# Keys, queries and the pooling's inputs made with x stationary and turned by DMA, the pooling's product and the gate weights in wider matmuls, and the last mixing slab later

## The chip, the core and the metric

One core of a Trainium2 chip runs the kernel. The metric is the device time of one execution in microseconds (us), median of three runs: 1546.35 us before (1546.16 to 1546.65). Some 0.2% of that, 3.1 us, is about what a measurement can tell from no change.

## What is computed

One layer on x of 256 tokens by 2048 channels, in float32. One input projection feeds three branches and their gates; each branch is projected, gated, summed, projected again, and normalised with x:

```python
proj = x @ w_in                        # 2048 -> pu, pz, sx, sz, sB, sC, sdt, mq, mk, mv, mo, mz, mi, mf, gates
y_pool  = pool_mixer(pu, w_pool, pool_scale) * silu(pz)
y_ssm   = mamba2_branch(sx, sz, sB, sC, sdt, ...)
y_mlstm = mlstm_branch(mq, mk, mv, mo, mi, mf, mz, ...)
g = sigmoid(gates + b_gate)            # 3 x 2048 per token
merged = sum(g[b] * (y[b] @ w_branch[b]) for b in range(3))
out = layer_norm(ALPHA * x + merged @ w_out)
```

The pooling has four groups of 512 channels. Group g takes the causal mean over w = 2, 4, 8 or 16 tokens less the token itself, and multiplies it with a 512 x 512 matrix of its own (w_pool). The mLSTM has eight heads of 256 channels, done here in four pairs, and needs keys and queries with channels on the partitions.

## The kernel before

All weights stream from HBM once, in an order written out by `stream()`; nearly all of the work is the product of x (256 tokens) or of a branch's output with slabs of 512 weight columns by 2048 rows (16 steps k of 128 rows). Each float32 operand is split into a high and a low float32r part: ScalarE (ACT) casts the high part (`split`, L190), VectorE (DVE) subtracts for the low part (L191), and TensorE (PE) sums high x high, high x low and low x high. The weights are split in parts of 1024 elements per partition, two steps k of a 512-column slab or four of a 256-column half. Four such parts fit (`hpool`, 4 buffers), so ACT and DVE may run up to four parts ahead of PE, and no further. Each engine works its own queue strictly in order.

There are two ways to make a slab. `slab_tok` (L262 to L264) keeps 128 tokens of x stationary and streams 512 weight columns: per k and token tile three matmuls of 512 columns, 96 in a slab; tokens come out on the partitions. `slab_chan` (L280 to L299) keeps 128 weight columns stationary: per k and block a matmul of 256 columns (low weights, L286) and one of 512 (high weights, high and low x side by side, L291), 128 in a slab; channels come out on the partitions, and ACT and DVE add the two halves (L298, L299). Before, keys and queries (`mlstm`) and the pooling's pu and pz (`pool`) are made by `slab_chan`, 16 slabs, and so are six slabs of the SSM branch. `slab_pool` (L301) mixes a pooling group in 48 matmuls of 256 columns and two PSUM tiles. `prep` makes the 48 small gate columns in 48 matmuls of 256 columns (L379 to L381).

Work beside the slabs is written as generators in the queue `pending`. `pump()` advances the oldest generator by one step; a slab calls it after every part, and whatever the step issues goes into the engines' queues there. `turned_parts` is such a generator: ACT copies a [256 x 512] float32 tile into its two 16-bit planes (L334, two copies), ACT issues two DMA transposes (L337), DVE puts the planes together again (L345, four copies), and the result is split. It runs seven times before (four mLSTM outputs, three merged tiles).

The PSUM pool `acc` has four tiles of one bank. A slab takes two of them, and gets a tile only when its last reader is done. The SBUF pool `big` has 11 tiles (names `t`).

In `pool`, group g makes pu (`slab_chan`), pools it on DVE (L698 adds, doubling the window each time, so 1, 2, 3 and 4 adds for the four groups; then L704 to L707), makes pz (`slab_chan`, then Silu), splits the pooled tile, and then mixes the group before it (`mix`, `slab_pool`, L684 on DVE). The last group is mixed at the end of `pool`, ahead of the merge's first gate slab.

Of the kernel before, what the change touches and what calls it, by code (L numbers as in the profile page):

```python
# [9 lines left out]
F32 = mybir.dt.float32  # L10
# [5 lines left out]
P = 128  # L16
# [22 lines left out]
def stream():  # L39


    def tok(c0, j):
        return [("w_in", 0, c0 + j * CB, CB, KT)]

    def chan(c0, j):
        return [("w_in", 0, c0 + j * CB + c, HB, KT) for c in (0, HB)]

    def merge(b):
        order = tok(GATES + b * D, 0)
        for j in range(NB):  # L50
            if j + 1 < NB:
                order += tok(GATES + b * D, j + 1)
            order.append(("w_branch", b, j * CB, CB, KT))
        return order

    order = tok(SZ, 0) + chan(SB_, 0) + chan(SC_, 0) + chan(SX, 0)
    for g in range(1, 4):
        order += tok(SZ, g) + chan(SX, g)
    order += merge(1)
    for g in range(4):  # L60
        order += chan(MK, g) + chan(MQ, g) + tok(MV, g) + tok(MO, g) + tok(MZ, g)
    order += merge(2)
    for g in range(4):
        order += chan(PU, g) + chan(PZ, g)
        if g:
            order.append(("w_pool", g - 1, 0, CB, CB // P))
    order.append(("w_pool", 3, 0, CB, CB // P))
    order += merge(0)
    order += [("w_out", 0, j * CB, CB, KT) for j in range(NB)]
    return order  # L70

# [6 lines left out]
def trunk(  # L78
# [31 lines left out]
    def nm(s):  # L110
        uid[0] += 1
        return f"{s}_{uid[0]}"
# [28 lines left out]
    def bank():  # L141
        return mx.tile([P, 512], F32, tag="mx", name=nm("mx"))
# [46 lines left out]
    def split(h, l, src):  # L189
        A.copy(h, src)  # L190
        V.tensor_sub(l, src, h)  # L191
# [64 lines left out]
    def yparts(ys):  # L256
        return lambda k: (ys[k // 4][0][:, k % 4, :], ys[k // 4][1][:, k % 4, :])
# [8 lines left out]
    def slab_tok(parts=xparts, first=False):  # L266
# [34 lines left out]
    def slab_pool(ph, pl):  # L301

        nk = CB // P
        ps = [acc.tile([P, 2, S], F32, tag="acc", name=nm("acc")) for _ in range(2)]
        for k, wh, wl in w_parts(nk):
            h, l = ph[:, k, :], pl[:, k, :]
            for c in range(4):
                o = ps[c // 2][:, c % 2, :]
                m = slice(c * P, (c + 1) * P)
                nc.tensor.matmul(o, lhsT=wh[:, m], rhs=h, start=k == 0 and c % 2 == 0, stop=False, skip_group_check=True)  # L310
                nc.tensor.matmul(o, lhsT=wh[:, m], rhs=l, start=False, stop=False, skip_group_check=True)  # L311
                nc.tensor.matmul(o, lhsT=wl[:, m], rhs=h, start=False, stop=k == nk - 1, skip_group_check=True)  # L312
            if k % 2 == 1:
                pump()
        return ps

    def transposed_parts(src_of, yh, yl):

# [5 lines left out]
            A.copy(yh[:, :, c], pt)  # L324
            V.tensor_sub(yl[:, :, c], pt, yh[:, :, c])

    def turned_parts(src, planes, yh, yl):
# [12 lines left out]
        yield  # L340
        f = planes.rearrange("p t c -> p (t c)").rearrange("p (a s) -> p a s", a=4)
        fv = f.bitcast(U16).rearrange("p a (t c h) -> p h t a c", t=NT, h=2)
        for i in range(2):
            for t in range(NT):
                V.tensor_copy(fv[:, i, t], dv[:, i, t])  # L345
            yield
        A.copy(yh, f)
        V.tensor_sub(yl, f, yh)

    def y_tiles():  # L350
        return (ypool.tile([P, 4, S], F32R, tag="yh", name=nm("yh")),
# [17 lines left out]
        return tiny.tile([P, NT, 40], F32, tag="s80", name=nm("s80"))  # L369

    def prep():
        wsh, wsl = t4([KT, 48], F32R), t4([KT, 48], F32R)
        split(wsh, wsl, wsm)
        yield
        yield
        yield
        pz = bank()[0:48, 0:S]
        for k in range(KT):
            nc.tensor.matmul(pz, lhsT=wsh[:, k, :], rhs=xh[:, k, :], start=k == 0, stop=False)  # L379
            nc.tensor.matmul(pz, lhsT=wsh[:, k, :], rhs=xl[:, k, :], start=False, stop=False)  # L380
            nc.tensor.matmul(pz, lhsT=wsl[:, k, :], rhs=xh[:, k, :], start=False, stop=k == KT - 1)  # L381
        zr = t2([S])
        A.copy(zr[0:48, :], pz)
        yield
        yield
        pzt = bank()[:, 0:96].rearrange("p (t c) -> p t c", t=NT)
        for t in range(NT):
            nc.tensor.transpose(pzt[:, t, :], zr[0:48, t * P:(t + 1) * P], ident[0:48, 0:48])
        V.tensor_tensor(out=zz, in0=pzt, in1=rowb[:, 0:48].unsqueeze(1).broadcast_to([P, NT, 48]), op=ALU.add)
# [257 lines left out]
    def mlstm():  # L647
        ys = []
        dw, dw1 = [t4([4, S]), t4([4, S])], t4([NM, P])
        pending.append(ml_weights(dw, dw1))  # L650
        for hp in range(4):
            kt, qt = t4([4, S]), t4([4, S])
            slab_chan(kt, MD ** -0.5)
            slab_chan(qt)
            ps = slab_tok()
            vh, vl = t4([NT, 2, MD + 2], F32R), t4([NT, 2, MD + 2], F32R)
            one = ones[:, 0:NT * 2 * 2].rearrange("p (t h d) -> p t h d", t=NT, h=2)
            V.tensor_copy(vh[:, :, :, MD:MD + 2], one)
# [12 lines left out]
            V.tensor_tensor(out=sz, in0=sz, in1=nw.unsqueeze(1).broadcast_to([P, NT, CB]), op=ALU.mult)  # L671
            pending.append(ml_pair(hp, kt, qt, vh, vl, so, sz, dw, dw1, ys))
        return ys


    def pool():
        ys = []
        pend = []

        def mix(g, ph, pl, sp):  # L680
            ps = slab_pool(ph, pl)
            yf = t4([4, S])
            for c in range(4):
                V.scalar_tensor_tensor(out=yf[:, c, :], in0=ps[c // 2][:, c % 2, :], scalar=pscale[:, 4 * g + c:4 * g + c + 1],  # L684
                                       in1=sp[:, c, :], op0=ALU.mult, op1=ALU.mult)
            yh, yl = y_tiles()
            split(yh, yl, yf)
            ys.append((yh, yl))

        for g, w in enumerate(WINDOWS):  # L690
            u = t4([4, 272])
            V.memset(u[:, :, 0:16], 0.0)
            slab_chan(u[:, :, 16:272])
# [6 lines left out]
            sp = t4([4, S])  # L700
            slab_chan(sp)
            A.activation(sp, sp, AF.Silu)
# [5 lines left out]
            ph, pl = t4([4, S], F32R), t4([4, S], F32R)  # L708
            split(ph, pl, p)
            if pend:  # L710
                mix(*pend.pop())
            pend.append((g, ph, pl, sp))
        mix(*pend.pop())
        return ys


    merged = []
# [7 lines left out]
        A.activation(sg, sg, AF.Sigmoid)  # L725
        return sg

    def merge(b, ys, done=None):
        sg = gate(b, 0)
        for j in range(NB):  # L730
            nxt = gate(b, j + 1) if j + 1 < NB else None
            ps = slab_tok(yparts(ys))
            if len(merged) <= j:
                m = ypool.tile([P, NT, CB], F32, tag="m", name=nm("m"))
# [23 lines left out]
            transposed_parts(lambda t, i: m[:, t, i * P:(i + 1) * P], mh, ml)  # L758
        yield

    merge(0, pool(), finish)


    st = const.tile([P, NT, 2 * NB, 6], F32, name="st")
# [146 lines left out]
```

## Time and profile before

| | before |
|---|---|
| median of 3 runs | 1546.35 us (1546.16 to 1546.65) |
| the profiled execution | 1545.71 us, of which the span from first to last instruction is 1543.8 us |
| PE busy | 1535.6 us, 99% of the span, 7727 matmuls |
| DVE busy | 964.8 us, 62% |
| ACT busy | 725.8 us, 47% |
| granted TensorE clock | 0.999 of 2.4 GHz |
| DMA | 305.35 MB, mean 198 GB/s |

Busy time of PE overlaps its neighbours in the records, since one matmul begins before the record of the last ends; the distance from one matmul's start to the next is what it costs. Waits of an engine are idle time before an instruction, put down to what came last.

### The profile page before, as it was taken

The page shows a single profiled execution, that of the slowest core. Times are in us where ns is not written, and L with a number is a line of the kernel's source. Part 1 is how long each engine was busy: PE and PEld are TensorE (multiplying, and loading weights), DVE is VectorE, ACT ScalarE, POOL GpSimd, SP SyncE. Part 2 cuts the span into 40 slices and gives each one's busy share as a digit, 9 for nine tenths or more (in the row PEclk, how much of TensorE's full clock was granted, in tenths as well). Part 3 has the DMA queues.
Part 4 walks back from the last instruction along what each step waited for, and adds up shares of the span by engine and source line. Part 5 has one row for each costly group of instructions (what it writes and reads, how often), then busy time and mean ns, then how long its engine had stood idle before and what let it go on. Part 6 is the DMA issues. An engine that isn't in the chain of part 4 may idle for free.

```text
span 1543.8 us, 19035 instructions
## 1 busy us (share of the span) xinstructions
PE 1535.6 (99%) x7727; PEld 1302.3 (84%) x7727; DVE 964.8 (62%) x1230; ACT 725.8 (47%) x818; POOL 13.6 (1%) x38
## 2 busy tenths in 40 slices
PE   9999999999999999999999999999999999999998
PEld 7888888888888888888888888888888898888886
DVE  5858888755754465465475466455666685556666
ACT  6545545544544444444444454443544454444441
POOL 0000000000000000000000000000000000000001
PEclk9999999999999999999999999999999999999999
DMA  8545555645655545546556556555555555566752
GB/s 316 192 168 187 208 189 187 229 173 191 218 191 192 191 172 205 195 173 210 196 182 208 191 204 212 199 197 196 188 191 189 191 191 191 193 224 213 273 198 99
DMA packets 70711, 305.35 MB, mean 198 GB/s; under 512 B 20280, under 2 KB 29152, under 8 KB 36832
## 3 DMA queue, kind: packets, MB, share of 16 engines
q1 hardware_dynamic: 55264, 299.69, 54.3%
q10 hardware_dynamic: 15360, 4.46, 1.6%
q8 instruction: 60, 0.98, 0.2%
q14 instruction: 27, 0.22, 0.0%
HBM read 298.32 MB, written 2.14 MB: 195 GB/s over the span
## 4 chain that ended last, share of the span: by engine, by line
PE 99%; DMA 1%; DVE 0%; issue 0%; DVEq 0%; SPq 0%
PE acc L291 21%; PE acc L262 21%; PE acc L264 21%; PE acc L263 21%; PE acc L286 11%; PE mx L527 1%; PE acc L312 0%; PE acc L311 0%; PE acc L310 0%; PE mx L597 0%; DMA w<-in_wt_dram 0%; PE mx L322 0%; DMA xf<-in_xT_dram 0%; PE mx L599 0%; PE mx L503 0%; PE mx L520 0%
## 5 line engine op out<-in xcount | busy, mean ns | idle before, releaser
L191 DVE TENSOR_TENSOR wl<-w,wh 128x1024 fp32r<-128x1024 f32 (+1 forms) x538 | 654.5, 1220 | 500.1 <-ACT wh L190 498.3
L190 ACT CAST wh<-w 128x1024 fp32r<-128x1024 f32 (+1 forms) x538 | 562.2, 1047 | 682.0 <-PE acc L264 449.6
L291 PE MATMUL acc<-xhl,wh 128*128 128x512 f32 x1408 | 488.2, 392 | 0.0
L286 PE MATMUL acc<-xhl,wl 128*128 128x256 f32 x1408 | 387.9, 281 | 0.0
L262 PE MATMUL acc<-wh,xhl 128*128 128x512 f32 x896 | 350.5, 391 | 0.3 <-ACT wh L190 0.3
L263 PE MATMUL acc<-wl,xhl 128*128 128x512 f32 x896 | 349.1, 390 | 0.2 <-DVE wl L191 0.2
L264 PE MATMUL acc<-wh,xhl 128*128 128x512 f32 x896 | 349.1, 390 | 0.1
L291 PEld LDWEIGHTS acc<-xhl,wh 128*128 128x128 f32 x1408 | 262.1, 188 | 54.3
L286 PEld LDWEIGHTS acc<-xhl,wl 128*128 128x128 f32 x1408 | 264.6, 188 | 3.5
L262 PEld LDWEIGHTS acc<-wh,xhl 128*128 128x128 f32 x896 | 168.2, 188 | 35.6 <-ACT wh L190 1.2
L264 PEld LDWEIGHTS acc<-wh,xhl 128*128 128x128 f32 x896 | 168.2, 188 | 35.5 <-DVE xhl L191 0.4
L263 PEld LDWEIGHTS acc<-wl,xhl 128*128 128x128 f32 x896 | 168.3, 188 | 35.3 <-DVE wl L191 1.0
L262 PE MATMUL acc<-wh,yh 128*128 128x512 f32 x384 | 149.7, 390 | 0.0
L264 PE MATMUL acc<-wh,yl 128*128 128x512 f32 x384 | 149.5, 389 | 0.0
L263 PE MATMUL acc<-wl,yh 128*128 128x512 f32 x384 | 149.5, 389 | 0.0
L264 PEld LDWEIGHTS acc<-wh,yl 128*128 128x128 f32 x384 | 72.1, 188 | 15.0
L262 PEld LDWEIGHTS acc<-wh,yh 128*128 128x128 f32 x384 | 72.1, 188 | 14.9
L263 PEld LDWEIGHTS acc<-wl,yh 128*128 128x128 f32 x384 | 72.1, 188 | 14.9
L298 ACT ACTIVATE t<-acc 128x256 f32<-128x256 f32 x88 | 31.8, 383 | 51.9 <-PE acc L291 51.9
L262 PE MATMUL acc<-wh,t 128*128 128x512 f32 (+1 forms) x144 | 52.7, 366 | 0.0
L264 PE MATMUL acc<-wh,t 128*128 128x512 f32 (+1 forms) x144 | 52.7, 366 | 0.0
L263 PE MATMUL acc<-wl,t 128*128 128x512 f32 (+1 forms) x144 | 52.6, 366 | 0.0
(202 smaller groups left out, 835.0 us busy)
## 6 DMA issues: line engine op xcount, KB each, us to landing
w<-in_wt_dram SPq DMA_DIRECT2D x264, 1024.0 KB, 4.8
t<-sc_a SPq DMA_DIRECT2D x8, 512.0 KB, 7.7
w<-in_wt_dram SPq DMA_DIRECT2D x6, 512.0 KB, 7.7
t<-in_b_gate_dram SPq DMA_DIRECT2D x12, 256.0 KB, 4.7
h<-in_x_dram SPq DMA_DIRECT2D x4, 512.0 KB, 4.8
xf<-in_xT_dram SPq DMA_DIRECT2D x7, 256.0 KB, 7.5
out_dram<-h SPq DMA_DIRECT2D x5, 256.0 KB, 2.5
w<-in_wt_dram SPq DMA_DIRECT2D x4, 256.0 KB, 4.8
```

The source lines that it names most:

```text
L190: A.copy(h, src)
L191: V.tensor_sub(l, src, h)
L262: nc.tensor.matmul(o, lhsT=h[:, c], rhs=wh, start=first, stop=False)
L263: nc.tensor.matmul(o, lhsT=h[:, c], rhs=wl, start=False, stop=False)
L264: nc.tensor.matmul(o, lhsT=l[:, c], rhs=wh, start=False, stop=last)
L286: nc.tensor.matmul(ps[c][:, 0, :], lhsT=wl[:, m], rhs=xh[:, k, :], start=False, stop=False, skip_group_check=True)
L291: nc.tensor.matmul(ps[c], lhsT=wh[:, m], rhs=xhl[:, k], start=first, stop=last, skip_group_check=True)
L298: A.mul(o, ps[c][:, 1, :], scale)
L527: nc.tensor.matmul(py[:, h * HP:(h + 1) * HP], lhsT=lt[c][:, h, :], rhs=xd[:, c, h, :], start=True, stop=True)
```

## The change

Keys and queries of each pair of heads, and pu and pz of each pooling group, are made by `slab_tok`; ACT copies PSUM to SBUF (`slab_turned`; pz goes through Silu there), and the generator `turned` turns the tile to channels on the partitions by way of two DMA transposes. The pz slab pumps after every k (`dense`), twice as often as before. The pooling of a group becomes a generator, `windows`, which runs during the pz slab. `slab_pool` takes high and low of the pooled tile side by side, as `slab_chan` does with x: 32 matmuls in place of 48, all four k for one block of 128 columns and then the next, in four PSUM tiles in place of two. `prep` keeps the high and low gate weights side by side as 96 stationary columns: 32 matmuls in place of 48, and one more add. The mixing of the last group moves from the end of `pool` to behind the merge's second gate slab, and its weights move in the stream with it.

```diff
     for g in range(4):
-        order += chan(MK, g) + chan(MQ, g) + tok(MV, g) + tok(MO, g) + tok(MZ, g)
+        order += tok(MK, g) + tok(MQ, g) + tok(MV, g) + tok(MO, g) + tok(MZ, g)
...
-            if k % 2 == 1:
+            if k % 2 == 1 or dense:
                 pump()
...
+    def slab_pool(phl, use):
         nk = CB // P
+        ws = list(w_parts(nk))
+        for c in range(4):
+            ps = acc.tile([P, 2, S], F32, tag="acc", name=nm("acc"))
+            m = slice(c * P, (c + 1) * P)
+            for k, wh, wl in ws:
+                hl = phl[k // 2][:, k % 2]
...
+                nc.tensor.matmul(ps, lhsT=wh[:, m], rhs=hl, start=k == 0, stop=k == nk - 1, skip_group_check=True)
...
+            use(c, ps)
...
+    def slab_turned(scale=1.0, func=AF.Copy, dense=False):
+        ps = slab_tok(dense=dense)
+        src, planes = t4([NT, CB]), t4([NT, CB])
+        for t in range(NT):
+            A.activation(src[:, t, :], ps[t], func, scale=scale)
+        return src, planes
...
         for hp in range(4):
-            kt, qt = t4([4, S]), t4([4, S])
-            slab_chan(kt, MD ** -0.5)
-            slab_chan(qt)
+            kq = []
+            for scale in (MD ** -0.5, 1.0):
+                src, planes = slab_turned(scale)
+                kq.append(by_channel(planes))
+                pending.append(turned(src, planes, kq[-1]))
...
+            def use(c, ps):
+                o, w = yf[:, c, :], pscale[:, 4 * g + c:4 * g + c + 1]
+                A.copy(o, ps[:, 1, :])
+                V.tensor_add(o, ps[:, 0, :], o)
+                V.scalar_tensor_tensor(out=o, in0=o, scalar=w, in1=sp[:, c, :], op0=ALU.mult, op1=ALU.mult)
...
+        for g, w in enumerate(WINDOWS):
+            phl, ready = [], []
+            pending.append(windows(w, slab_turned(), phl))
+            zs = slab_turned(func=AF.Silu, dense=True)
+            pending.append(gates(*zs, ready))
             if pend:
                 mix(*pend.pop())
```

Three places show what moves. The first is ACT's queue at the end of the last pz slab, where the third group is mixed (names `t` are SBUF tiles, `acc` PSUM tiles, `wh` weight parts). Before:

```order
L298 ACTIVATE t_1530_9766<-acc_9857 128x256
L298 ACTIVATE t_1530_9766<-acc_9858 128x256
L190 CAST wh_10057<-w_10027 128x1024
L702 ACTIVATE t_1530_9766<-t_1530_9766 128x1024
L190 CAST wh_10100<-w_10098 128x1024
L190 CAST wh_10116<-w_10098 128x1024
```

and now:

```order
L191 CAST wh_9506<-w_9504 128x1024
L191 CAST t_1544_9403<-t_1540_9387 128x2x256
L191 CAST t_1545_9412<-t_1540_9387 128x2x256
L369 ACTIVATE t_1548_9431<-acc_9265 128x512
L369 ACTIVATE t_1548_9431<-acc_9266 128x512
L191 CAST wh_9523<-w_9504 128x1024
L715 COPY t_1550_9435<-acc_9446 128x256
L342 COPY t_1549_9432<-t_1548_9431 128x1024 x2
L715 COPY t_1550_9435<-acc_9458 128x256
L345 DMA_TRANSPOSE t_1548_9431<-t_1549_9432 128x8x128
L715 COPY t_1550_9435<-acc_9471 128x256
L345 DMA_TRANSPOSE t_1548_9431<-t_1549_9432 128x8x128
```

The readers of the slab's PSUM tiles (L369) now stand behind the split of the pooled tile, and the readers of the mixing's PSUM tiles (L715) between copies and transposes; one more L715 and the cast of the next part follow.

The second is DVE's queue in the last pz slab (window 16). Before, each add stood between two weight parts:

```order
L698 TENSOR_TENSOR t_1526_9758<-t_1501_9576 128x4x271
L191 TENSOR_TENSOR wl_9834<-w_9811,wh_9833 128x1024
L698 TENSOR_TENSOR t_1527_9760<-t_1526_9758 128x4x269
L191 TENSOR_TENSOR wl_9862<-w_9859,wh_9861 128x1024
L698 TENSOR_TENSOR t_1528_9762<-t_1527_9760 128x4x265
```

and now they come after the copies that wait for the transposes:

```order
L352 COPY t_1523_9279<-t_1516_9261 128x4x128 x2
L192 TENSOR_TENSOR wl_9370<-w_9347,wh_9369 128x1024
L352 COPY t_1523_9279<-t_1516_9261 128x4x128 x2
L192 TENSOR_TENSOR wl_9394<-w_9391,wh_9393 128x1024
L732 TENSOR_TENSOR t_1531_9345<-t_1523_9279 128x4x271
L732 TENSOR_TENSOR t_1535_9359<-t_1531_9345 128x4x269
L192 TENSOR_TENSOR wl_9416<-w_9391,wh_9415 128x1024
L732 TENSOR_TENSOR t_1536_9367<-t_1535_9359 128x4x265
L192 TENSOR_TENSOR wl_9439<-w_9436,wh_9438 128x1024
L732 TENSOR_TENSOR t_1539_9379<-t_1536_9367 128x4x257
L192 TENSOR_TENSOR wl_9443<-w_9436,wh_9442 128x1024
```

The copies stand one part behind their transposes here, and two adds share one part.

The third is PE's queue in a mixing slab, one block of 128 columns. Before:

```order
L310 MATMUL acc_9956<-t_1489_9503,wh_9960 128x256
L311 MATMUL acc_9956<-t_1490_9504,wh_9960 128x256
L312 MATMUL acc_9956<-t_1489_9503,wl_9961 128x256
```

for each k and block; now the whole of a block is

```order
L318 MATMUL acc_9446<-t_1473_9008,wh_9438 128x512
L313 MATMUL acc_9446<-t_1473_9008,wl_9439 128x256 x2
L318 MATMUL acc_9446<-t_1473_9008,wh_9438 128x512
L313 MATMUL acc_9446<-t_1477_9023,wl_9443 128x256
L318 MATMUL acc_9446<-t_1477_9023,wh_9442 128x512
L313 MATMUL acc_9446<-t_1477_9023,wl_9443 128x256
L318 MATMUL acc_9446<-t_1477_9023,wh_9442 128x512
L318 MATMUL acc_9458<-t_1473_9008,wh_9438 128x512
```

and the next block takes the next PSUM tile.

## Rows read from the trace of the kernel before

**Rows 1.** The page: busy time of each engine, and the chain that ended last.

```profile
PE 1535.6 (99%) x7727; PEld 1302.3 (84%) x7727; DVE 964.8 (62%) x1230; ACT 725.8 (47%) x818; POOL 13.6 (1%) x38
...
PE 99%; DMA 1%; DVE 0%; issue 0%; DVEq 0%; SPq 0%
```

**Rows 2.** Waits: engine, tile and line, what it waited for, total us, times, longest.

```profile
ACT wh L190 <- PE acc L264: 449.6, 273, 3.8
...
ACT wh L190 <- PE acc L291: 158.1, 100, 2.8
...
PE mx L154 <- DVE warm L151: 1.3, 1, 1.3
...
PE mx L812 <- ACT t L810: 0.9, 1, 0.9
```

**Rows 3.** Windows of a chan slab, a tok slab, and half a chan slab with a mixing.

```profile
core 0: us, PE busy (x) PEld busy (x) DVE busy (x) ACT busy (x) POOL busy (x), PEclk, DMA share, GB/s
1187.02:1209.21 22.19, 22.19 (x130) 19.54 (x129) 17.16 (x19) 10.59 (x13) 0.00 (x0) 1.00 0.53 186
1314.28:1336.04 21.76, 21.76 (x97) 18.02 (x97) 11.00 (x12) 9.39 (x9) 0.00 (x0) 1.00 0.54 193
1209.21:1226.06 16.85, 16.85 (x114) 15.52 (x113) 10.92 (x14) 8.90 (x10) 0.00 (x0) 1.00 0.51 189
```

**Rows 4.** One line of `prep`: duration in ns, first and last start in us.

```profile
L380 PE MATMUL mx<-xhl,t x16: 276/276/279, 76.1 to 81.2; 128*48 128x256 f32 x16
```

**Rows 5.** ACT in order of time around three pairs of DMA transposes (start, us).

```profile
582.18 1.05 ACT L190 CAST wh<-w 128x1024 fp32r<-128x1024 f32 x1
582.31 2.73 ACTq L337 DMA_TRANSPOSE t<-t  x2
585.13 1.05 ACT L190 CAST wh<-w 128x1024 fp32r<-128x1024 f32 x1 [1.90 <-issue]
...
926.97 3.33 ACTq L337 DMA_TRANSPOSE t<-t  x2
...
1340.51 1.05 ACT L190 CAST wh<-w 128x1024 fp32r<-128x1024 f32 x1
1340.63 4.73 ACTq L337 DMA_TRANSPOSE m<-t  x2
1345.40 3.06 ACT L190 CAST wh<-w 128x1024 fp32r<-128x1024 f32 x3 [3.85 <-PE acc L264]
```

**Rows 6.** DVE in order of time: the copies behind these transposes.

```profile
589.86 1.47 DVE L345 COPY t<-t 128x512 uint16<-128x512 uint16 x4 [0.62 <-DMA t<-t]
...
936.71 1.47 DVE L345 COPY t<-t 128x512 uint16<-128x512 uint16 x4 [4.05 <-DMA t<-t]
...
1347.63 0.47 DVE L345 COPY t<-m 128x512 uint16<-128x512 uint16 x1
```

**Rows 7.** DMA issues by line: KB or kind, median us to landing.

```profile
t<-t ACTq DMA_TRANSPOSE x8, 5.9
...
m<-t ACTq DMA_TRANSPOSE x6, 5.6
```

**Rows 8.** DVE in order of time in the third pu and pz slabs.

```profile
1188.24 1.29 DVE L698 TENSOR_TENSOR t<-t 128x1084 f32<-128x1084 f32 x1
1189.44 1.22 DVE L191 TENSOR_TENSOR wl<-w,wh 128x1024 fp32r<-128x1024 f32 x1
1190.58 1.27 DVE L698 TENSOR_TENSOR t<-t 128x1076 f32<-128x1076 f32 x1
...
1197.91 1.18 DVE L704 SCALAR_TENSOR_TENSOR t<-t,t 128x992 f32<-128x992 f32 x1
```

**Rows 9.** Groups of instructions: count, busy us, mean ns, idle before.

```profile
L298 ACT ACTIVATE t<-acc 128x256 f32<-128x256 f32 x88 | 31.8, 383 | 51.9 <-PE acc L291 51.9
...
L334 ACT COPY t<-t 128x1024 uint16<-128x1024 uint16 x8 | 8.0, 1044 | 4.2 <-DVE t L640 4.1
...
L190 ACT CAST xhl<-xf 128x512 fp32r<-128x512 f32 (+1 forms) x10 | 5.2, 530 | 2.1 <-DMA xf<-in_xT_dram 2.0
...
L552 ACT ACTIVATE t<-acc 128x512 f32<-128x512 f32 x8 | 4.7, 597 | 4.1 <-PE acc L264 3.9
```

More of the change, by code (lines that the diff above doesn't have):

```diff
@@ L46, in chan, with merge @@
         return [("w_in", 0, c0 + j * CB + c, HB, KT) for c in (0, HB)]
-    def merge(b):
+    def merge(b, between=()):
         order = tok(GATES + b * D, 0)
@@ L52, in merge @@
                 order += tok(GATES + b * D, j + 1)
+            if j == 0:
+                order += between
             order.append(("w_branch", b, j * CB, CB, KT))
@@ L264, in mm_tok, with slab_tok @@
         nc.tensor.matmul(o, lhsT=l[:, c], rhs=wh, start=False, stop=last)
-    def slab_tok(parts=xparts, first=False):
+    def slab_tok(parts=xparts, first=False, dense=False):
         ps = [acc.tile([P, CB], F32, tag="acc", name=nm("acc")) for _ in range(NT)]
@@ L299, in slab_chan, with low @@
                 V.scalar_tensor_tensor(out=o, in0=ps[c][:, 0, :], scalar=scale, in1=o, op0=ALU.mult, op1=ALU.add)
-    def slab_pool(ph, pl):
+    def slab_pool(phl, use):
         nk = CB // P
[L304 to L313, printed above, removed]
+        ws = list(w_parts(nk))
[4 more added lines that the diff above has]
+                hl = phl[k // 2][:, k % 2]
+                def low():
+                    nc.tensor.matmul(ps[:, 0, :], lhsT=wl[:, m], rhs=hl[:, 0, :], start=False, stop=False,
+                                     skip_group_check=True)
+                if k:
+                    low()
+                nc.tensor.matmul(ps, lhsT=wh[:, m], rhs=hl, start=k == 0, stop=k == nk - 1, skip_group_check=True)
+                if not k:
+                    low()
+            use(c, ps)
+            if c % 2 == 1:
                 pump()
-        return ps
     def transposed_parts(src_of, yh, yl):
@@ L346, in turned_parts, with by_channel @@
             yield
+    def by_channel(t):
+        return t.rearrange("p t c -> p (t c)").rearrange("p (a s) -> p a s", a=4)
+    def turned_parts(src, planes, yh, yl):
+        f = by_channel(planes)
+        yield from turned(src, planes, f)
         A.copy(yh, f)
         V.tensor_sub(yl, f, yh)
+    def slab_turned(scale=1.0, func=AF.Copy, dense=False):
[4 more added lines that the diff above has]
+        return src, planes
     def y_tiles():
@@ L371, in prep @@
     def prep():
-        wsh, wsl = t4([KT, 48], F32R), t4([KT, 48], F32R)
-        split(wsh, wsl, wsm)
+        ws = [t4([KT // 2, 2, 48], F32R) for _ in range(2)]
+        for i, w in enumerate(ws):
+            split(w[:, :, 0, :], w[:, :, 1, :], wsm[:, i * KT // 2:(i + 1) * KT // 2, :])
         yield
@@ L678, in pool, with mix @@
         pend = []
-        def mix(g, ph, pl, sp):
-            ps = slab_pool(ph, pl)
+        def mix(g, phl, sp, ready):
+            assert ready
             yf = t4([4, S])
-            for c in range(4):
-                V.scalar_tensor_tensor(out=yf[:, c, :], in0=ps[c // 2][:, c % 2, :], scalar=pscale[:, 4 * g + c:4 * g + c + 1],
-                                       in1=sp[:, c, :], op0=ALU.mult, op1=ALU.mult)
+            def use(c, ps):
[3 more added lines that the diff above has]
+                V.scalar_tensor_tensor(out=o, in0=o, scalar=w, in1=sp[:, c, :], op0=ALU.mult, op1=ALU.mult)
+            slab_pool(phl, use)
             yh, yl = y_tiles()
@@ L688, in mix, with windows @@
             ys.append((yh, yl))
-        for g, w in enumerate(WINDOWS):
+        def windows(w, us, phl):
             u = t4([4, 272])
             V.memset(u[:, :, 0:16], 0.0)
-            slab_chan(u[:, :, 16:272])
+            yield from turned(*us, u[:, :, 16:272])
             s, n = u, 1
@@ L707, in pool, with gates @@
             V.tensor_sub(p[:, :, 0:w], p[:, :, 0:w], u[:, :, 16:16 + w])
-            ph, pl = t4([4, S], F32R), t4([4, S], F32R)
-            split(ph, pl, p)
+            yield
+            for i in range(2):
+                t = t4([2, 2, S], F32R)
+                phl.append(t)
+                split(t[:, :, 0, :], t[:, :, 1, :], p[:, 2 * i:2 * i + 2, :])
+                yield
+        def gates(src, planes, ready):
+            yield from turned(src, planes, by_channel(planes))
+            ready.append(True)
+        for g, w in enumerate(WINDOWS):
[3 more added lines that the diff above has]
+            pending.append(gates(*zs, ready))
             if pend:
                 mix(*pend.pop())
-            pend.append((g, ph, pl, sp))
-        mix(*pend.pop())
-        return ys
+            pend.append((g, phl, by_channel(zs[1]), ready))
+        return ys, lambda: mix(*pend.pop())
     merged = []
@@ L726, in gate, with merge @@
         return sg
-    def merge(b, ys, done=None):
+    def merge(b, ys, done=None, between=None):
         sg = gate(b, 0)
@@ L731, in merge @@
             nxt = gate(b, j + 1) if j + 1 < NB else None
+            if j == 0 and between is not None:
+                between()
             ps = slab_tok(yparts(ys))
@@ L759, in finish @@
         yield
-    merge(0, pool(), finish)
+    ys, last = pool()
+    merge(0, ys, finish, last)
     st = const.tile([P, NT, 2 * NB, 6], F32, name="st")
```

34 lines of the change are left out of this document (17 added, 17 removed).

## The prediction

> **What bounds the kernel now.** I read the page's first part and its chain first: PE is busy 99% of the span and holds 99% of the chain that ended last [rows 1]. Then the waits: PE waits a few microseconds in all, the longest of them at the start (1.3 us) and in the last normalisation (0.9 us), while ACT waits 449.6 + 158.1 us for PE to give a buffer of split weights back [rows 2]. So the weights are ready early, and the time is the sum of the distances between matmuls. Whatever takes matmul time out is gained in full, as long as PE still never waits. How long PE can be left alone follows from the four split buffers: a buffer comes back three parts before its next use, a part of a 512-column slab lasts 21.76 / 8 = 2.72 us [rows 3], and the cast and the subtraction take 1.05 and 1.22 us [rows 5, 8]; so a part lies ready about 3 x 2.72 - 1.05 - 1.22 = 5.9 us before PE needs it (an estimate from those rows). A delay on ACT or DVE below that costs nothing; a PSUM tile that is read late costs at once.
>
> **What PE saves.** The profiled execution took 1545.71 us, 0.64 us under the median of 1546.35; the sum is made in it and laid on the median.
>
> A slab with weight columns stationary takes 22.19 us, one with x stationary 21.76 us, both windows holding nothing else on PE [rows 3]. Both stream the same columns, and the first has 128 matmuls against 96, so each matmul has a fixed part. Sixteen slabs change: 16 x 0.43 = 6.9 us. The same code makes 28 such slabs already, so I see no reason for another price; 6.5 to 7.2 us.
>
> A mixing takes 16.85 - 22.19 / 2 = 5.76 us [rows 3]. Its new step, a matmul of 512 and one of 256 columns with a new stationary operand each, is what the 22.19 us slab consists of 64 times: 0.347 us. Sixteen steps are 5.55 us; four mixings save 0.8 us.
>
> `prep`: the second of its three matmuls starts from 76.1 to 81.2 us, sixteen times, so three take 5.1 / 15 = 0.34 us and one 0.113 us [rows 4]. Sixteen go: 1.8 us. The 96-column ones may cost up to the 0.12 us of a mixing's matmul (5.76 / 48), which takes 0.1 us back.
>
> Together 9.5 us, with ends 8.8 and 9.9. Without any new wait the median is 1536.9 us.
>
> The Trainium skill speaks against this first term: "TensorE: Matmul & The Clock Gate", section Back-to-back issue gap, gives N / 2.4 + 2.5 ns for the distance of matmuls at full clock. By that a 512-column matmul takes 215.8 ns and a slab 20.7 us in either form, and the sixteen slabs would save 1.3 us in all. The trace disagrees: 21.76 / 96 is 227 ns.
>
> **What is added, and what covers it.** 16 slabs get a turn each: on ACT two copies of 1.04 us [rows 9] and two issues of a DMA transpose, on DVE four copies of 1.47 us together [rows 6], against the four PSUM reads on either engine that go. Averaged over 21.76 us both engines have room: in the window of the tok slab DVE is busy 11.00 and ACT 9.39 us [rows 3]. What counts is how long a turn holds a queue. ACT's next cast came 2.8, 3.4 and 4.8 us after the first of two transposes (the third: 1345.40 - 1340.63) [rows 5], and DVE's copies began 7.5, 9.7 and 7.0 us after it [rows 5, 6]; one transpose lands after 5.6 to 5.9 us in the median [rows 7].
>
> *Keys and queries.* In the mLSTM the copies stand three parts, 8.2 us, behind the first transpose. With 7.0 to 9.7 us to land, DVE waits 1.5 us at most, out of a lead of 5.9. The first products of keys and queries come a whole step later still. I take nothing; if another delay has used the lead up, each of eight turns could cost that 1.5 us, 12 us, which no row suggests.
>
> *The pz slabs.* Here the pump runs twice per part, and the copies stand only one part behind. I walk through the last group (window 16), in us from the end of the pu slab. ACT reads PSUM (two of 0.6 us [rows 9], the first before the slab's end), casts, copies (to 3.8), and issues the transposes at 3.8. The first lands at 9.6 and the second at 11.3 (7.5 after the issue). DVE: two copies to 10.3, a weight part (1.14 us from one start to the next [rows 8]) to 11.4, two copies to 12.1, a part to 13.3, two adds (1.20 each [rows 8]) to 15.7, a part to 16.8, an add to 18.0, a part to 19.2, an add to 20.4, a part to 21.5, and the pooled tile (1.18 [rows 8] and two small ones) to 23.1. PE needs those parts at 13.6, 16.3, 19.0, 21.8 and 22.5, so it just never waits: the smallest margin is 1.0 us, for the mixing's second part, which the new loop needs 0.7 us into the slab.
>
> *The mixing slabs.* Behind the pooled tile ACT splits it (two of 0.5 us [rows 9], to 24.1), and only then reads the pz slab's PSUM tiles (to 24.7 and 25.2). The mixing now takes four PSUM tiles, and its third, due at 21.76 + 2 x 1.39 = 24.5, is the one being read: 0.2 us of waiting. Behind that ACT has a cast (26.2), the first block's read (0.38 [rows 9], 26.6), two copies (28.5), the second block's read (28.9), the two transposes with the other reads between (free at 31.4 or 33.4, for 2.8 or 4.8 us) and the last read; the next weight part but one is cast by 32.8 or 34.8 and subtracted by 34.0 or 36.0. PE ends the mixing at 27.6; the next slab's PSUM tiles are those of the first two blocks, free after DVE's add at 27.8 and 29.3 where 27.6 and 28.5 are due: 0.2 + 0.8 us. Its third part is due at 34.3: 0 or 1.7 us. In sum 1.3 to 3.0 us. For window 8 there is one add less (1.2 us) and one cast more (1.0 us) ahead of the PSUM reads: 1.1 to 2.8 us. For window 4 the split is done before the slab ends, and all stands 2.4 us earlier: 0 to 0.3 us. Together 2.4 to 6.1 us; I take the middle, **4.3 us**, since the issue held ACT 2.8 us in one of the rows and 4.8 in another. With the late landing of 9.7 us windows 8 and 16 lose 2.2 us more each, 10.5 us at most.
>
> *The rest.* The last mixing stands behind a gate slab, whose PSUM readers are first in DVE's queue, and its result is needed only 12 steps k into the merge slab; nothing else is turned there. I take nothing, at most 1 us. Adds, splits and pumps that move within DVE's queue are in the walk above. The SP queue keeps its order but for one slab of weights.
>
> **The sum.** -6.9 - 0.8 - 1.8 + 4.3 = -5.2 us: 1540.5 us by the profiled execution, **1541.2 us** by the median.
>
> **The rivals.**
>
> *No waits at all* (chance 0.21): the transposes land early, or the chains run shorter than I walk them, and under 2 us come back: 1536.9 to 1538.9. For it: PE waits nowhere now though seven turns run [rows 2], and the third turn in rows 5 and 6 held ACT longest and still cost PE nothing. Against it: none of the seven stands before a PSUM tile that PE needs.
>
> *The gain is given back* (0.17): landing as late as 9.7 us in the pz slabs, or the long hold of ACT with lost leads after it, 7 to 12.6 us: 1543.9 to 1549.4.
>
> *Slower* (0.10): one mechanism, the third PSUM tile of the mixing. Its reader stands behind the pooled tile, which stands behind the landing of the second transpose. Each microsecond of landing beyond 7.5 us moves the windows of 8 and 16 by one each, and from 2.6 us on that of 4 as well. With 6.1 us of waits as the base, 12.6 us are passed where 2 d + (d - 2.6) = 6.5, d = 3.0, so from a landing 10.5 us after the issue. The longest in the rows is 9.7 us; ordinary weight loads and 32 more transposes share the queues, so it is not excluded. At 11.2 us the time is some 1551.
>
> *Columns alone set PE's time* (0.02): then the slabs and mixings save nothing, since each form streams the same columns, only the 16 matmuls of `prep` go (1.8 us), and with the waits of 4.3 us the time is 1548.9. The windows of 22.19 and 21.76 us speak against it. The rule of the Trainium skill cited above comes close to this.
>
> **How the numbers follow.** The forecast, 2 to 7 us of waits, 1538.9 to 1543.9, has 0.50. A difference under 0.2% (3.1 us, about what a measurement of this kernel can tell from no change) is the same. Faster, below 1543.3: 0.21 + 0.42 of the forecast, 0.63. Same: 0.08 of the forecast, 0.16 of the gain given back, 0.02: 0.26. Slower: 0.11. The range leaves out the slower rival and the far end of what is given back, and takes in the best case: 1536.9 to 1548.0.
>
> **What the profile of the changed kernel would show.** Right: PE's matmuls in the pu, pz, key and query slabs at 227 ns; windows of a pu slab of 21.76 us and a mixing of 5.55 us plus its waits; new waits of PE for ACT (L369) and DVE (L716) on `acc`, a few tenths to 2 us each, for windows 8 and 16 only; none in the mLSTM. Wrong: waits of PE for DVE on `wl` in the pz slabs or behind keys and queries, transposes that land after 10 us, or a mixing for window 2 or 4 that waits as long as that for 16.

## The result: slower by 0.96%, and where the profile after shows it

| | before | after |
|---|---|---|
| median | 1546.34 us (4 runs, 1546.16 to 1546.65) | 1560.32 us (4 runs, 1557.60 to 1565.55) |
| after / before | | 1.0096, 95% interval 1.0083 to 1.0108 |
| profiled execution | 1545.71 us | 1557.60 us |

The forecast was 1541.2 us. The ratio is the recorded estimate over the runs; the medians alone give 1.0090. The runs of after lie 8 us apart, those of before half a microsecond: something in after happens by chance.

The page of after, its first part and its chain of work (as in [rows 1]):

```profile
PE 1534.6 (99%) x7135; PEld 1275.6 (82%) x7135; DVE 967.4 (62%) x1252; ACT 749.8 (48%) x835; POOL 13.6 (1%) x38
...
PE 89%; DMA 4%; DVE 3%; ACT 2%; issue 1%; ACTq 1%; POOL 0%; DVEq 0%; SPq 0%; POOLq 0%
```

592 matmuls are gone and PE's busy time is only 1.0 us less, where the forecast took 9.5 us out: some of the rest took longer. And a tenth of the chain isn't PE's any more. The waits of after (engine, tile and line, what it waited for, total us, times, longest; as in [rows 2]):

```profile
DVE t L352 <- DMA t<-t: 53.1, 13, 10.8
ACT wh L191 <- issue: 47.0, 21, 8.9
ACT wh L191 <- DVE t L352: 16.6, 2, 11.0
...
PE acc L264 <- DVE wl L192: 10.6, 5, 4.6
...
PE acc L318 <- ACT t L369: 0.8, 2, 0.5
PE acc L263 <- DVE t L716: 0.7, 2, 0.3
```

PE now waits 4.6 us in one piece, for split weights; the forecast had put waits of tenths to 2 us in the pooling alone. PE in order of time around the longest wait, which lies in the second mLSTM pair:

```profile
610.12 0.39 PE L263 MATMUL acc<-wh,xhl 128*128 128x512 f32 x1
615.15 0.80 PE L264 MATMUL acc<-wl,xhl 128*128 128x512 f32 x1 [4.64 <-DVE wl L192]
...
735.90 0.51 PE L264 MATMUL acc<-wl,xhl 128*128 128x512 f32 x1 [4.22 <-DVE wl L192]
```

DVE was not slow; it stood at the copies (L352) behind the keys' transposes:

```profile
600.52 1.23 DVE L192 TENSOR_TENSOR wl<-w,wh 128x1024 fp32r<-128x1024 f32 x1 [0.42 <-ACT wh L191]
612.53 1.46 DVE L352 COPY t<-t 128x512 uint16<-128x512 uint16 x4 [10.78 <-DMA t<-t]
```

And ACT meanwhile, with the keys' transposes at 596.43 and 597.82 and the queries' pair at 602.41 (as in [rows 5]):

```profile
596.43 1.25 ACTq L345 DMA_TRANSPOSE t<-t  x1
...
597.82 1.48 ACTq L345 DMA_TRANSPOSE t<-t  x1
...
602.41 11.84 ACTq L345 DMA_TRANSPOSE t<-t  x2
614.35 2.94 ACT L191 CAST wh<-w 128x1024 fp32r<-128x1024 f32 x3 [11.01 <-DVE t L352]
```

SP's queue loads 1 MB of weights twice in that time, 2.2 and 5.4 us after the first transpose:

```profile
598.63 0.33 SPq L228 DMA_DIRECT2D w<-in_wt_dram  x1
...
601.78 0.33 SPq L228 DMA_DIRECT2D w<-in_wt_dram  x1
```

The windows of after (columns as in [rows 3]; the last three are the granted clock, the DMA share and GB/s) show what became of these transfers, what the waits cost, and the pooling:

```profile
core 0: us, PE busy (x) PEld busy (x) DVE busy (x) ACT busy (x) POOL busy (x), PEclk, DMA share, GB/s
596.00:600.00 4.00, 4.00 (x20) 3.30 (x19) 2.34 (x2) 2.96 (x4) 0.00 (x0) 1.00 1.04 316
600.00:604.00 4.00, 4.00 (x19) 3.30 (x18) 1.33 (x2) 3.33 (x4) 0.00 (x0) 1.00 1.51 95
600.10:601.70 1.60, 1.60 (x8) 1.32 (x8) 1.18 (x2) 1.60 (x3) 0.00 (x0) 1.00 3.34 119
604.00:608.00 4.00, 4.00 (x19) 3.34 (x18) 0.00 (x0) 0.00 (x0) 0.00 (x0) 1.00 0.77 118
...
615.10:620.30 5.20, 5.15 (x12) 4.11 (x13) 4.84 (x7) 2.24 (x4) 0.00 (x0) 0.50 0.58 203
...
608.00:624.00 16.00, 11.36 (x40) 8.87 (x39) 9.57 (x15) 5.46 (x7) 0.00 (x0) 0.79 0.80 244
728.00:744.00 16.00, 11.78 (x45) 9.22 (x44) 9.60 (x15) 5.49 (x7) 0.00 (x0) 0.89 0.80 232
...
1079.31:1101.07 21.76, 21.76 (x97) 18.03 (x96) 12.01 (x12) 8.89 (x9) 0.00 (x0) 1.00 0.55 194
...
1166.35:1171.98 5.63, 5.63 (x33) 4.92 (x32) 4.12 (x8) 4.55 (x8) 0.00 (x0) 1.00 0.70 252
1215.67:1222.06 6.39, 6.04 (x33) 4.77 (x31) 4.80 (x8) 5.65 (x9) 0.00 (x0) 1.00 0.46 165
1267.98:1274.42 6.44, 5.99 (x34) 4.79 (x32) 5.58 (x10) 4.71 (x8) 0.00 (x0) 1.00 0.49 163
1320.43:1326.05 5.62, 5.62 (x33) 4.92 (x32) 4.76 (x9) 3.48 (x6) 0.00 (x0) 1.00 0.57 207
```

From 600 to 608 us the DMA engines are busy at shares of 1.51 and 0.77 (a share over 1 means packets that overlap), and move 95 and 118 GB/s where 316 went just before. The rate is down from 600.1 us on, before the load of 601.78 is issued. Both kinds suffer: the loads of 598.63 and 601.78 land after 12.0 and 12.7 us, where a median load takes 4.8, and the keys' second transpose lands 14.7 us after its issue, the longest of all:

```profile
DMA to landing us min/median/max: 3.0/6.0/14.7
```

With each of the two stalls the granted clock falls to 0.50 (1.2 GHz), and it stays there for a while when PE works again. Behind the first stall PE makes 12 matmuls in 5.20 us, where the full clock makes 23. So each stall costs twice. The two windows of 16 us hold 40 and 45 matmuls; in g2_sync_kq below, without the stalls, they hold 73 and 72. (33 + 27) x 0.227 = 13.6 us.

### The profile page after: what moved, and what is told of

It reads as the page before. It is cut to its first block, busy times and chain, and to the rows that moved or that the text cites. A ratio compares the mean times of both kernels' runs of the same rounds, so it can differ in the third digit from the quotient of the medians.

```text
span 1555.5 us, 17953 instructions
## 1 busy us (share of the span) xinstructions
PE 1534.6 (99%) x7135; PEld 1275.6 (82%) x7135; DVE 967.4 (62%) x1252; ACT 749.8 (48%) x835; POOL 13.6 (1%) x38
## 4 chain that ended last, share of the span: by engine, by line
PE 89%; DMA 4%; DVE 3%; ACT 2%; issue 1%; ACTq 1%; POOL 0%; DVEq 0%; SPq 0%; POOLq 0%
PE acc L264 26%; PE acc L265 26%; PE acc L263 26%; PE acc L292 6%; DMA t<-t 3%; PE acc L287 3%; DVE wl L192 1%; PE mx L553 1%; ACT wh L191 1%; ACT t L342 1%; ACTq L345 1%; DVE t L732 1%; PE acc L318 0%; DMA w<-in_wt_dram 0%; PE mx L623 0%
## 5 line engine op out<-in xcount | busy, mean ns | idle before, releaser
L264 PE MATMUL acc<-wl,xhl 128*128 128x512 f32 x1408 | 550.9, 391 | 10.6 <-DVE wl L192 10.6
L263 PE MATMUL acc<-wh,xhl 128*128 128x512 f32 x1408 | 553.3, 393 | 1.7 <-DVE t L716 0.7
L265 PE MATMUL acc<-wh,xhl 128*128 128x512 f32 x1408 | 550.5, 391 | 0.1
L264 PEld LDWEIGHTS acc<-wl,xhl 128*128 128x128 f32 x1408 | 265.6, 189 | 67.2 <-DVE wl L192 12.9
L263 PEld LDWEIGHTS acc<-wh,xhl 128*128 128x128 f32 x1408 | 265.5, 189 | 59.4 <-ACT wh L191 2.6
L265 PEld LDWEIGHTS acc<-wh,xhl 128*128 128x128 f32 x1408 | 265.4, 188 | 55.8 <-DVE xhl L192 0.4
L292 PE MATMUL acc<-xhl,wh 128*128 128x512 f32 x384 | 133.7, 392 | 0.0
L287 PE MATMUL acc<-xhl,wl 128*128 128x256 f32 x384 | 106.1, 281 | 0.0
L292 PEld LDWEIGHTS acc<-xhl,wh 128*128 128x128 f32 x384 | 71.7, 188 | 14.8
L287 PEld LDWEIGHTS acc<-xhl,wl 128*128 128x128 f32 x384 | 72.2, 188 | 0.9
L352 DVE COPY t<-t 128x512 uint16<-128x512 uint16 x80 | 31.4, 454 | 53.1 <-DMA t<-t 53.1
```

Of the source, the lines that this page charges most:

```text
L263: nc.tensor.matmul(o, lhsT=h[:, c], rhs=wh, start=first, stop=False)
L287: nc.tensor.matmul(ps[c][:, 0, :], lhsT=wl[:, m], rhs=xh[:, k, :], start=False, stop=False, skip_group_check=True)
L292: nc.tensor.matmul(ps[c], lhsT=wh[:, m], rhs=xhl[:, k], start=first, stop=last, skip_group_check=True)
```

## The experiments

The theories as they stand in the expectations: A, keys' and queries' turns follow each other too closely; B, the pooling makes the loss; C and E, turns land late beside weight loads or at this place, whatever their distance and order; D, casts between the transposes release loads at the wrong moment; F, transposes of one queue and loads of another, under way together, can slow each other, by chance; G, the keys' turn comes while the loads are still making up for the turn before.

| run | median us (range, runs) | ratio to before, 95% |
|---|---|---|
| e1_kq_chan | 1546.28 (1545.48 to 1547.31, 10) | 1.0002, 0.9993 to 1.0011 |
| e2_q_spaced | 1564.38 (1563.82 to 1570.08, 4) | 1.0116, 1.0099 to 1.0133 |
| e3_kq_only | 1568.52 (1558.08 to 1572.07, 4) | 1.0133, 1.0095 to 1.0171 |
| e4_pool_late | 1558.88 (1545.17 to 1563.49, 10) | 1.0065, 1.0035 to 1.0094 |
| f1_together | 1556.56 (1549.67 to 1562.88, 6) | 1.0067, 1.0042 to 1.0093 |
| f2_parity | 1561.61 (1555.84 to 1564.66, 4) | 1.0087, 1.0067 to 1.0106 |
| f3_between | 1545.98 (1545.54 to 1546.86, 10) | 1.0000, 0.9990 to 1.0009 |
| f4_parity_late | 1553.80 (1538.89 to 1562.66, 10) | 1.0031, 1.0004 to 1.0058 (without the run of 1562.66) |
| g1_later | 1543.61 (1543.21 to 1544.69, 10) | 0.9984, 0.9975 to 0.9993 |
| g2_sync_kq | 1543.86 (1543.43 to 1545.71, 10) | 0.9986, 0.9977 to 0.9996 |
| g5_sync_all_late | 1537.45 (1536.97 to 1537.69, 4) | 0.9944, 0.9929 to 0.9959 |
| g6_sync_kq_late | 1538.02 (1537.47 to 1541.11, 6) | 0.9943, 0.9924 to 0.9961 |

**Which part loses.** e1 takes the keys and queries out of the changed kernel; e3 puts them alone into the kernel before.

```diff
-        order += tok(MK, g) + tok(MQ, g) + tok(MV, g) + tok(MO, g) + tok(MZ, g)
+        order += chan(MK, g) + chan(MQ, g) + tok(MV, g) + tok(MO, g) + tok(MZ, g)
...
+            kt, qt = t4([4, S]), t4([4, S])
+            slab_chan(kt, MD ** -0.5)
+            slab_chan(qt)
```

> Keys and queries go back to slab_chan (weights stationary, nothing turned); the pooling, its mixing and prep stay changed. Theory A (the turns of keys and queries, two pairs of transposes some 6 us apart, starve PE twice in the mLSTM, by 7.2 and 6.1 us with the half clock behind them): those stalls go, the 3.4 us that eight slabs save go too, and what is left is 1546.3 - 3.4 - 0.8 - 1.8 + 5.2 (the pooling's waits) = 1545.5 us, 1544 to 1547. Theory B (the loss is made by the pooling's PSUM tiles that are read late): the time stays at 1556 us or more.

> The kernel before with keys and queries alone made by slab_tok and turned; pooling, mixing and prep as before. Theory A: 1546.3 - 3.4 + 13.3 (the two stalls with the half clock behind them) = 1556 us, 1551 to 1562. Theory B: the eight cheaper slabs alone show, 1542.9 us, 1541 to 1545.

e1 came to 1546.28, in A's range and within 2 us over ten runs; e3 came to 1568.52, above A's range, with 14 us between its runs. The keys and queries make the whole loss and the spread; B falls. e3 lost more than expected: in its profile three turns stall and not two.

**Spacing.** In after the queries' copies stand three to four weight parts further ahead in ACT's queue than the place where the pump issues them. e2 pins them there:

```diff
-            A.copy(pv[:, i], sv[:, i])
+            keep(A.copy(pv[:, i], sv[:, i]))
...
-                pending.append(turned(src, planes, kq[-1]))
+                pending.append(turned(src, planes, kq[-1], tc.keep_in_program_order))
```

> Only the place of the turns of keys and queries in ACT's queue changes: their copies keep the place at which the pump issues them, so the queries' transposes follow the keys' by about seven parts (19 us) and not by 6 us. Theory A: each pair lands after 6 to 9 us as the others do, PE waits nowhere in the mLSTM, TensorE keeps its full clock there, and only the pooling's 5.2 us of waits are left over the 1536.9 us without waits: 1542 us, 1540 to 1545. Theory C (transposes land late whenever weight loads run beside them, whatever their distance): landing stays at 11 to 15 us in some pairs, and the time at 1553 us or more.

A miss: 1564.38 us. The queries' pair stood 22.5 us behind the keys', and the keys' alone still starved PE, in all three later pairs. The windows of e2 behind the keys' transposes at 597.06 and 598.45, and ACT's next cast:

```profile
599.00:603.00 4.00, 4.00 (x19) 3.33 (x18) 2.69 (x3) 1.93 (x3) 0.00 (x0) 1.00 1.50 136
603.00:607.00 4.00, 4.00 (x20) 3.30 (x19) 0.00 (x0) 1.71 (x2) 0.00 (x0) 1.00 1.07 93
```

```profile
615.67 1.04 ACT L191 CAST wh<-w 128x1024 fp32r<-128x1024 f32 x1 [9.30 <-DMA w<-in_wt_dram]
```

Theory A falls, and what C forecast came. The rate is as low as in after, at shares over 1, and here ACT waits 9.30 us for the weights themselves: the transfers are slow, not the queue of ACT. Its long hold at the issue in after goes with slow transfers and doesn't make them.

**The order of casts and transposes.** In the three slow turns ACT's queue reads cast, transpose, cast, transpose; in the others no cast stands between the transposes. f1 issues both without a pump between; f2 puts one pump step ahead; f3 puts a cast between the transposes of the kernel before.

```diff
 f1:
-            yield
+            if not together:
+                yield
 f2:
+        for _ in range(later):
+            yield
 f3:
+            tc.keep_in_program_order(
+                nc.scalar.dma_start_transpose(...))
+            for _ in range(2 if i == 0 else 1):
+                yield
```

> The changed kernel with the two transposes of each key or query turn issued without a pump, and so without a cast, between them (the turn keeps its length in pumps). In the changed kernel the three slow turns are those of the keys of pairs 2 to 4, where ACT's queue reads: cast of a second half, transpose, cast, transpose, cast; two loads of 1 MB of weights are then released 2.2 and 5.2 us after the first transpose, and the DMA rate falls from 390 to some 50 to 130 GB/s for ten microseconds. Theory D (two weight loads released while a pair of transposes is under way make all of them slow): the second load is released later, at 6 to 7 us as behind the mLSTM outputs' turns, the second transpose lands within 10 us of its issue, and the time is 1542 us, 1540 to 1548. Theory E (turns at this place of the mLSTM land late whatever the order of issue): 1553 us or more.

> The changed kernel with one more pump step ahead of each key and query turn, so that the keys' first transpose follows the cast of a first half of a weight load and not of a second. Theory D: as in the pooling and in the first pair, the next load is released 7 us after the first transpose, both land within 8 us, PE waits nowhere in the mLSTM, and with the pooling's 5.2 us of waits the time is 1542 us, 1540 to 1545. Theory E: 1553 us or more.

> The kernel before, with one cast of a weight part put between the two transposes of each of its turns that have room for it (three mLSTM outputs: cast of a second half, transpose, cast of a first half, transpose; three merged tiles: the halves the other way round). Nothing else changes. Theory D: where a second load is released within some 3 us of the first while the transposes run, they land after 10 us or more and PE waits up to 5 us in the mLSTM: up to 1546.1 + 3 x 7 = 1567 us, at least 1549. If the order of casts and transposes alone is harmless: 1546 us, within 1 us.

f1 1556.56, f2 1561.61, f3 1545.98: D falls from both sides, and E's times came. Changing the order doesn't free the slow turns, and a cast between the transposes harms nothing where the turn was well before. In the profile of f1 one of the three keys' turns landed 11.1 us after its first transpose, another after 16.7, in the same order of issue: chance has a part in it.

The profiles of f1 and f2 also show that a second load close by isn't what makes a turn slow. In f1, in the turn that landed after 11.1 us, the second load was issued at 603.45, 6.6 us behind the first transpose, and the rate was down before that:

```profile
600.00:603.40 3.40, 3.40 (x17) 2.81 (x16) 2.34 (x2) 3.40 (x4) 0.00 (x0) 1.00 1.18 113
```

In f2 the two loads beside the keys' turns were issued 5.3 to 5.4 us apart, as far as loads stand in the mean (two parts of 2.72), and the second transposes still landed 16.4, 16.5 and 10.4 us after their issue.

**Place and queue.** What was left is when the turn runs and on which queue. g1 moves the turns of keys and queries four pump steps later; g2 leaves them where they are and issues their transposes on SP's queue, among the weight loads.

```diff
 g1:
+        for _ in range(later):          # 4
+            yield
...
+            keep(A.copy(pv[:, i], sv[:, i]))
 g2:
-            nc.scalar.dma_start_transpose(out=dv[:, i].rearrange("p t a c -> p (t a) c"),
+            queue.dma_start_transpose(out=dv[:, i].rearrange("p t a c -> p (t a) c"),
...
+                pending.append(turned(src, planes, kq[-1], nc.sync))
```

> The changed kernel with the turns of keys and queries four pump steps (11 us) later and their copies kept at that place. Theory G (the keys' turn stands 16 us behind that of the previous pair's output, while DVE and the weight loads still make up for its wait, so loads run beside the transposes 3.0 to 4.6 us apart and not 5.4): the loads have caught up, the transposes land within 10 us, and the time is 1542 us, 1540 to 1548. Theory F (whatever the loads' distance, a transposition that is under way together with a weight load of the other queue can slow both down many times over, by chance): the time stays above 1548 us, with large spread from run to run.

> The changed kernel with the transposes of keys and queries alone issued on SP's queue, the one that loads the weights, and not on ACT's. Theory F: packets of one queue go one transfer after the other, so that a transposition never runs beside a weight load; both take their usual 3 to 6 us, ACT isn't held at the issue, PE waits nowhere in the mLSTM, and the time is 1542 us, 1540 to 1546. If the two kinds hamper each other within one queue too: 1553 us or more, with large spread.

1543.61 and 1543.86 us: G's and F's numbers for the two came out, with at most 2.3 us between the ten runs of either and no stall and no half clock in the mLSTM of either profile. What F forecast for g1, more than 1548 us, did not come, and neither did E's slow turns at the old place in g2. In g2 the keys' transposes start at 596.77, at the same place, with the loads 2.7 and 7.5 us behind. Its windows and its landing:

```profile
600.00:604.00 4.00, 4.00 (x20) 3.30 (x19) 2.42 (x6) 2.55 (x3) 0.00 (x0) 1.00 1.04 279
604.00:608.00 4.00, 4.00 (x19) 3.34 (x18) 2.62 (x3) 1.46 (x2) 0.00 (x0) 1.00 1.02 274
...
608.00:624.00 16.00, 16.00 (x73) 13.24 (x72) 9.62 (x12) 7.08 (x9) 0.00 (x0) 1.00 0.77 236
728.00:744.00 16.00, 16.00 (x72) 13.27 (x71) 9.04 (x9) 7.20 (x8) 0.00 (x0) 1.00 0.59 202
```

```profile
DMA to landing us min/median/max: 3.1/5.8/7.5
```

In g1 the keys' transposes at 604.28 and 605.65 land after 3.7 and 3.4 us; the next load is issued at 607.96, 3.7 us behind the first transpose, when the two have nearly landed. The window of g1 over them:

```profile
604.00:608.00 4.00, 4.00 (x20) 3.30 (x19) 1.79 (x2) 1.60 (x3) 0.00 (x0) 1.00 1.07 323
```

So neither the number of transposes nor ACT's part of them costs anything; what cost time is transposes of ACT's queue that were under way together with loads of SP's queue, at the place of the keys of pairs 2 to 4. G's reason for that place isn't borne out. It is true that the turn of the previous pair's output has its copies on DVE only 6 us ahead, and that SP issues loads 3.0 to 4.6 us apart behind it in after. But f2's turns were slow with loads 5.3 to 5.4 us apart, and in f1 and in after the rate fell before the second load was issued. What g1 shows is that the turns are free 11 us later.

The DMA packets in the traces bear F's picture out in part (those of 4 bytes left out). In g2, from 599.0 to 600.5 us only packets of transposes start (256 bytes each, 1394 of them), and from 601.5 to 603.5 us only packets of loads (8 KB, 75): one transfer after the other. In after, from 601.0 to 603.5 us, 24 packets of either kind start, mixed. But mixing alone isn't slow: behind the previous output's turn, from 584.5 to 586.5 us, 96 and 97 start, mixed too.

That g2's loads come a little later (2.7 and 7.5 us behind the first transpose, against 2.2 and 5.4 in after) is not enough to explain why g2's turns are free, since f1's came 2.2 and 6.6 us behind.

The Trainium skill ("DMA: Bandwidth & Descriptors", section Issuing engines are not separate DMA queues) has all queues run on the same 16 DMA engines and interleave there, so that the choice of queue saves issue time only. The trace agrees with the interleaving, as packets of the two queues start mixed in after, and not with the consequence: with the queue alone changed, the median is 1560.32 - 1543.86 = 16.5 us lower.

One reservation stands. g1, g2 and g5 ran on one chip and g6 on a second; e1 to e4 ran on a third and f1 to f4 on a fourth, and for after none is recorded. No kernel known to stall in its turns has a run on record on the chips of the g runs. That it is the chip and not the queue or the place is unlikely, since two chips show no stall with the transposes of keys and queries on SP's queue and two show stalls with them on ACT's, but no run excludes it.

**The pooling.** e4 lets the pooled tile be split, and the gates turned, behind the readers of the PSUM tiles; f4 is f2 with that, g6 is g2 with it, and g5 is g6 with all transposes on SP's queue.

```diff
+            for _ in range(9 - w.bit_length() + 1):
+                yield
             for i in range(2):
                 t = t4([2, 2, S], F32R)
...
-                split(t[:, :, 0, :], t[:, :, 1, :], p[:, 2 * i:2 * i + 2, :])
+                tc.keep_in_program_order(A.copy(t[:, :, 0, :], p[:, 2 * i:2 * i + 2, :]))
+                V.tensor_sub(t[:, :, 1, :], p[:, 2 * i:2 * i + 2, :], t[:, :, 0, :])
...
-            pending.append(gates(*zs, ready))
             if pend:
                 mix(*pend.pop())
+            pending.append(gates(*zs, ready))
```

> The changed kernel, but the pooled tile is split behind the pz slab, and the turn of the gates is issued behind the mixing, so that the readers of the PSUM tiles come first in ACT's queue; the mLSTM is untouched. Theory A: the pooling's waits go (5.2 us), the mLSTM's stay: 1560.3 - 5.2 = 1555 us, 1551 to 1560. Theory B: 1545 us or less.

> The pump step of f2_parity together with the later split and the later turn of the gates of e4_pool_late. Theory D: neither the mLSTM nor the pooling waits, and what is left is the sum without waits, 1536.9 us, 1536 to 1540: faster than before by 0.6%. Theory E: 1550 us or more.

> As g2_sync_kq, but all transposes on SP's queue, and with the later split and the later turn of the gates of e4_pool_late. Theory F: neither the mLSTM nor the pooling waits: 1537 us, 1536 to 1540, with small spread. Otherwise, SP's queue stands behind a transposition that waits for its copies, weight loads start late, and PE waits for them: 1545 us or more.

> g2_sync_kq with the later split and the later turn of the gates, and nothing else: against g2_sync_kq (1543.9 us) it prices the pooling's waits by themselves, against g5_sync_all_late (1537.45 us) the queue of the other turns. If the pooling's waits are the 5.2 us of the changed kernel's trace and the queue matters only where loads are bunched: 1538.0 us, 1537 to 1539, and no wait of PE for ACT's L369 or DVE's L716 on acc. If the other turns on ACT's queue cost something too, it lies above 1539 us.

e4 came to 1558.88, in A's range, and f4 to 1553.80, in E's. They say little by their medians, since the mLSTM's chance covers 5 us; the lowest of f4's ten runs, 1538.89, is about what would remain when no turn is hit. g5 and g6 came out in the range forecast. g6 against g2 prices the pooling's waits by themselves: 1543.86 - 1538.02 = 5.8 us. The two were taken on different chips, where the medians of before were 1546.11 (g2) and 1546.54 (g6), so it is good to some 0.4 us. Two of the eleven runs of before taken beside g6 came to 1551.53 and 1553.82; no profile shows why. g5, 1537.45, beats before by 0.56%, and its waits of PE are all but those of the kernel before [rows 2]:

```profile
PE mx L155 <- DVE warm L152: 1.3, 1, 1.3
PE mx L862 <- ACT t L860: 0.9, 1, 0.9
PE acc L263 <- ACT wh L191: 0.7, 1, 0.7
PE acc L264 <- DVE wl L192: 0.2, 1, 0.2
```

Between g5 and g6 the runs tell no difference. g5 is the one to keep: all transposes stand in one queue there. The Trainium skill (the same page, section Silent corruption: two transposing streams in flight at once) warns that transposes of two queues can spoil each other's results; no run here shows that.

## Why the prediction was wrong

**What PE saves: right.** A pu slab takes 21.76 us, as forecast; a mixing without waits 5.63, where 5.55 was worked out; the sixteen steps of `prep` start from 76.2 to 79.7 us, 0.23 us apart where they were 0.34, which is 1.7 us of the 1.8. With every wait gone the forecast had 1536.9 us; g5 measured 1537.45. The rival of columns alone falls with that: by it g5 couldn't be below 1546.1 - 1.8 = 1544.3.

**The pooling: right, mis-sized by 1.5 us.** Waits stand at L369, at L716 and, the longest of them, at the third part behind the mixing (0.8 us each on `wl`), as walked: behind the pz slabs of windows 8 and 16 (mixings of 6.39 and 6.44 us) and not behind that of window 4 (5.63 us). 4.3 us were taken out of 2.4 to 6.1, and 5.8 were measured. A pair held ACT 4.6 to 5.2 us there, the upper end of [rows 5] and not their middle.

**Keys and queries: the step that failed.** "I take nothing" rested on two numbers. The copies were to stand 8.2 us behind the first transpose. The forecast's own rows said otherwise: less the waits that they show, DVE reached the copies at 589.86 - 0.62 = 589.24 and 936.71 - 4.05 = 932.66, 6.9 and 5.7 us behind it [rows 5, 6]. In after DVE reached the keys' copies at 612.53 - 10.78 = 601.75, 5.3 us behind it. This alone would cost nothing: with a landing at 9.7 us DVE waits 4.4, within the lead. The landing was bounded by 9.7 us, the longest in [rows 5, 6], and here the keys' second transpose landed 16.1 us after the first. The lead of 5.9 us was right: 10.78 - 5.9 = 4.9, and PE waited 4.64. The bound of 9.7 us is the step that failed: it came from turns at other places, and none of those rows has a landing slowed as these were. The forecast's sign of being wrong, transposes that land after 10 us, came with it. Its words "each of eight turns could cost that 1.5 us, 12 us, which no row suggests" named the place and then priced it from rows of another situation. The slower rival named the weight loads, which "share the queues" with the transposes; in fact they stand on two queues, SP's and ACT's, and with both on SP's (g2) the stalls were gone. Besides, no term stood for the clock: after a stall of 4.6 us PE runs at 1.2 GHz for 5.2 us more, 12 matmuls where 23 fit, 2.5 us.

The sum again: 1546.3 - 9.5 + 5.8 + 13.6 = 1556.2, against 1557.6 of the profiled execution; 1.4 us are not placed. The rival that ends slower had the right mechanism, a late landing, but in the pooling, where the pairs landed within 8.5 us of their first transpose.

**Open.** Why the two queues slow each other three times over, and by what a turn is hit or spared, no run here shows: the turns of the mLSTM's outputs meet one load as well and no profile shows one slowed past 10 us, and in the profile of f4 the first of the slow places was spared too (7.4 us) with loads 5.2 us apart. So the place of the keys of pairs 2 to 4 stays unexplained. After and g2 on one chip, and a third queue for the transposes, were not tried.

## What to carry to other kernels

Price a transfer by what else is on the DMA engines at the moment it will run: the longest landing seen at other places of a kernel is no bound for a new place, where it may meet loads of another queue. A chance stall shows in the spread of the runs before it shows in a median; and where a second queue for transfers isn't needed, try them in the one that carries the stream. A stall of PE that lets its clock fall costs more than its own length.

## What was not expected of the hardware

Two loads of 1 MB and two transposes of 256 KB, some 8 us of work at the 316 GB/s just before, ran at 95 and 118 GB/s where they met across two queues, and the loads landed after 12.0 and 12.7 us (in e2 after 16.3 and 15.7). The issue of a pair of transposes, mostly 2.6 to 5.2 us, held ACT 11.84 us while the transfers were slow. In the queue of the weight loads the transposes of keys and queries landed within 7.8 us (g2, g5 and g6, one profile each).
